# First block of a two-block kernel: S5 preparation on GpSimd, S5 scan between gate projections, convolution and mLSTM last

## The chip, the cores and the metric

The kernel runs on one core of a Trainium2 chip. The metric is the device time of one execution in microseconds (us). The core has five engines that each execute their own instructions in the order in which the program holds them: PE (TensorE, matmuls), DVE (VectorE), ACT (ScalarE), POOL (GpSimd) and SP (SyncE, here only DMA issues). An instruction that has to wait holds up everything behind it on its engine.

## The reference, cut to what matters

The program computes two transformer blocks for S = 256 tokens of width 1024. The change lies in the first third of the first block:

```
h    = rmsnorm(x)
u, q_in, k_in, v, o, i, f, gate = split(h @ w_in)
y_s5 = s5(u)                         # diagonal complex state space, 32 groups x 64 states
y_m  = mlstm(q_in, k_in, v, o, i, f) # q,k: causal convolution of 4 taps, silu; 4 heads, 2 chunks
merged = sigmoid(gate_s5) * (y_s5 @ w_br_s5) + sigmoid(gate_m) * (y_m @ w_br_m)
x = x + merged @ w_out               # then cross attention, FFN, and the second block

s5:  a_bar = exp(lam*dt);  b_bar = (a_bar-1)/lam * b      # depends on parameters alone
     states = associative_scan(a_bar, b_bar u);  y = gelu(Re(c states) + d u);  y * sigmoid(y @ w_glu)
mlstm: per head  p = (q k^T) * decay mask;  h = (w q C + p v) / max(|den|, exp(-m));  norm
```

So three branches (S5, mLSTM, gates) start from the same normalised input and meet in `merged`. Data lets them run in nearly any order.

## The kernel before, in words

**Products.** Every product with a weight matrix is made as three fp32r matmuls. SP loads a raw weight tile of 128 x 1024 (`wload`, L318), ACT rounds it to `hi` (L320), DVE takes `lo` = raw - hi (L321), and PE runs 24 matmuls of 128x256 on the pair (L328, L329, L330; with tokens on the partitions L337 to L339). So every weight tile costs an ACT, a DVE and 24 PE instructions. Four raw and three hi/lo buffers let the loads run ahead.

**Who sets the order.** The Tile scheduler puts each engine's instructions into one list, by the order of the source and by priorities, from simulated times. Weight loads have a raised priority (300), as has `s5_prep` (500).

**First block before.** `s5_prep` (L639 to L723) computes powers of a_bar and the coefficients from parameters, in some 110 small DVE instructions on 128x16 tiles, with two exponentials as POOL `pow` (L306). Then come the norm's statistics (squares, column sums on PE L454, a POOL `pow` `rmsr` L505, `row_bcast` on PE L498), the u projection (w_fm tiles, evacuated by `ev_u` with the factor `rs`), and `s5` (L725): for four groups of heads, outer products of coefficients and parameters (DVE L747 to L762 for `mb` and `w`, POOL L747 to L768 for `mc`, CR and CN), PE transposes (L772) and small matmuls `kp` (L777, L779), the input states (L795), a scan over 64 chunks by ten combine steps of five DVE instructions (L806 to L810), the output matmuls (L830). Program order goes on with the q/k projection and its convolution (`ev_qk`: per pair of tiles one DVE multiply L1646, two ACT instructions, six DVE steps L1654, an ACT tanh L1656, a DVE step L1657), the v, i, f and o projections, `mlstm` (L853 on: gate vectors, then per head scores L914 and L915, mask product `pT` L917, values L919 to L921, normalisation), the eight gate projections (`ev_g`, L1696 and L1698), `s5_glu` (L835, exact fp32 matmuls L424), the branch projections w_brs and w_brm, and w_out.

**Around it.** Since engines follow the lists, in the execution the S5 scan and the four mLSTM heads of DVE lie beside the gate projections of PE: of PE's rows, 27 to 48 gate matmuls stand between the steps of one head and the next.

Of the kernel before, what the change touches and what calls it, by code (L numbers as in the profile page):

```python
# [258 lines left out]
def _program(ctx, tc, nc, a, offs, dump):  # L259
# [379 lines left out]
    def s5_prep(bp):  # L639
        t16 = lambda tag, n=16: T(bp, [P, n], tag)  # L640
        lr, li, ldt = C["lr"], C["li"], C["ldt"]
        dt = pexp(ldt, [P, 16], "s5dt")
# [34 lines left out]
        pr = T(bp, [P, 16, 5], "pr")  # L677
        pi = T(bp, [P, 16, 5], "pi")
        G.memset(pr[:, :, 0:1], 1.0)
        G.memset(pi[:, :, 0:1], 0.0)  # L680
        ar, ai = pr[:, :, 1], pi[:, :, 1]

        def cmul(orr, oi, xr_, xi_, yr, yi):
            n_ = len(orr.shape) > 2 and orr.shape[2] or 1
            sh = list(orr.shape)
            t = [T(bp, sh, "cm%d_%d" % (n_, q_), bufs=2) for q_ in range(4)]
            tt(t[0], xr_, yr, op=mult)
            tt(t[1], xi_, yi, op=mult)
            tt(t[2], xr_, yi, op=mult)
            tt(t[3], xi_, yr, op=mult)  # L690
            tt(orr, t[0], t[1], op=sub)
            tt(oi, t[2], t[3], op=add)

        cs_, sn_ = t16("cs_"), t16("sn_")
        cmul(cs_, sn_, cn, sn, cq, sq)
        tt(ar, er, cs_, op=mult)
        tt(ai, er, sn_, op=mult)
        den, a1 = t16("den"), t16("a1")
        tt(den, lr, lr, op=mult)
        tt(z, li, li, op=mult)  # L700
        tt(den, den, z, op=add)
        V.reciprocal(den, den)
        nli = t16("nli")
        ts(nli, li, -1.0, None, op0=mult)
        cmul(pr[:, :, 2], pi[:, :, 2], ar, ai, ar, ai)
        sq2 = lambda X: bc(X[:, :, 2:3], [P, 16, 2])
        ts(a1, ar, -1.0, None, op0=add)
        cr = T(bp, [P, 16, 4], "cr")
        ci = T(bp, [P, 16, 4], "ci")
        cmul(cr[:, :, 3], ci[:, :, 3], a1, ai, lr, nli)  # L710
        tt(cr[:, :, 3], cr[:, :, 3], den, op=mult)
        tt(ci[:, :, 3], ci[:, :, 3], den, op=mult)
        cmul(cr[:, :, 2], ci[:, :, 2], cr[:, :, 3], ci[:, :, 3], ar, ai)
        cmul(cr[:, :, 0:2], ci[:, :, 0:2], cr[:, :, 2:4], ci[:, :, 2:4], sq2(pr), sq2(pi))
        cmul(pr[:, :, 3:5], pi[:, :, 3:5], pr[:, :, 1:3], pi[:, :, 1:3], sq2(pr), sq2(pi))
        NL = 5
        akr, aki, akn = T(bp, [P, NL, 16], "akr"), T(bp, [P, NL, 16], "aki"), T(bp, [P, NL, 16], "akn")
        V.tensor_copy(akr[:, 0, :], pr[:, :, 4])
        V.tensor_copy(aki[:, 0, :], pi[:, :, 4])
# [4 lines left out]

    def s5(bp, b2, K5, U, prep):  # L725
        cr, ci, pr, pi, akr, aki, akn = prep
        NL = 5
# [14 lines left out]
        def outer(eng, xa, ya, xb, yb, nt, tag):  # L742
            sh = [P, 4, nt, 16]
            m = []
            for x_, y_ in ((xa, ya), (xb, yb)):
                t = T(bp, sh, tag + str(len(m)))
                eng.tensor_tensor(t, bc(x_[:, :, :, None], sh), bc(y_[:, :, None, :], sh), op=mult)  # L747
                m.append(t)
            return m

        halves = [(g, slice(64 * g, 64 * g + 64)) for g in range(2)]
        for b in range(4):
            s4 = slice(4 * b, 4 * b + 4)
            BR, BI = bt[b % 2][:, 0], bt[b % 2][:, 1]
            crb, cib, brb, bib = cr[:, s4, :], ci[:, s4, :], b_re[:, s4, :], b_im[:, s4, :]
            prb, pib, xrb, xib = pr[:, s4, :], pi[:, s4, :], c_re[:, s4, :], c_im[:, s4, :]
            m = outer(V, crb, brb, cib, bib, 4, "mb")
            for g, hs in halves:
                tt(BR[hs, :, :, g, :], m[0][hs], m[1][hs], op=sub)
            m = outer(V, crb, bib, cib, brb, 4, "mb")  # L760
            for g, hs in halves:
                stt(BI[hs, :, :, g, :], m[0][hs], -1.0, m[1][hs], op0=mult, op1=sub)  # L762
            c = outer(G, prb, xrb, pib, xib, 5, "mc")
            for g, hs in halves:
                G.tensor_tensor(CR[hs, s4, :, g, :], c[0][hs], c[1][hs], op=sub)
            c = outer(G, prb, xib, pib, xrb, 5, "mc")
            for g, hs in halves:
                G.tensor_tensor(CN[hs, s4, :, g, :], c[0][hs], c[1][hs], op=add)  # L768
            for src, dst in ((BR, VR), (BI, VI)):
                tr = T(pa, [P, 4, P], "a")  # L770
                for q in range(4):
                    PE.transpose(tr[:, q, :], src[:, q].rearrange("p t g h -> p (t g h)"), ident)  # L772
                ACT.copy(dst[:, s4, :], tr)
            kp = T(pa, [32, 4, P], "a")
            for q in range(4):
                fl = lambda X: X.rearrange("p g h -> p (g h)")
                mm(kp[:, q, :], fl(BR[:, q, 3]), CR[:, 4 * b + q, 0:4].rearrange("p t g h -> p (t g h)"),  # L777
                   start=True, stop=False)
                mm(kp[:, q, :], fl(BI[:, q, 3]), CN[:, 4 * b + q, 0:4].rearrange("p t g h -> p (t g h)"),  # L779
                   start=False, stop=True)  # L780
            for t in range(4):
                ACT.copy(KS[32 * t:32 * t + 32, s4, 32 * t:], kp[:, :, :P - 32 * t])

        us = T(dr, [16, 32, 4, 64], "us")
        U2 = T(bp, [P, 16, 64], "U2")
        nc.scalar.dma_start(us.rearrange("(a j) q t c -> (j q) a (t c)", a=4), U.rearrange("p a t c -> p a (t c)"))
        for t in range(4):
            nc.scalar.dma_start(U2[32 * t:32 * t + 32], us.rearrange("a q t c -> t q a c")[t])
        ST = T(bp, [P, 2, 16, 65], "ST")
        V.memset(ST[:, :, :, 0:1], 0.0)  # L790
        for b in range(4):
            vp = T(pa, [P, 2, 4, 64], "a")
            for r_, W in enumerate((VR, VI)):
                for q in range(4):
                    mm(vp[:, r_, q, :], W[:, 4 * b + q, :], U2[:, 4 * b + q, :], start=True, stop=True)  # L795
            ACT.copy(ST[:, :, 4 * b:4 * b + 4, 1:], vp)

        def combine(k, d0, n_):
# [1001 lines left out]
```

## Time and profile before

| | |
|---|---|
| median of 3 runs | 1218.24 us (1216.67 to 1220.58) |
| profiled execution | 1222.49 us, its span 1220.7 us, mean granted clock 0.980 |
| PE busy | 1175.4 us (96%) |
| DVE busy | 905.4 us (74%) |
| ACT busy | 681.7 us (56%) |
| POOL busy | 94.5 us (8%) in 94 instructions |
| chain that ended last | PE 82%, DVE 11% |

PE is the engine to watch: over the whole program it idles 45 us. The 40-slice line of the page shows where: its first two slices stand at 7 tenths, the slices after them at 9, and the granted clock falls under full speed in the third.

### The profile page before, as it was taken

How to read it: one execution, taken by the hardware profiler on the slowest of the kernel's cores; microseconds unless marked ns; L12 is line 12 of the kernel's file. 1: busy time of each engine (PE TensorE's matmuls, PEld its weight loads, DVE VectorE, ACT ScalarE, POOL GpSimd, SP SyncE). 2: the span in 40 equal slices, each digit the busy share in tenths (PEclk: the TensorE clock that was granted, in tenths of full speed). 3: DMA queues.
4: the chain of work that ended last, by engine and by line, in shares of the span. 5: the costliest groups of instructions: out<-in, count | busy, mean ns of one | idle time of the engine just before them, and what ended most of it. 6: DMA issues, size and time to landing. Idle time of an engine off the chain costs nothing.

```text
span 1220.7 us, 23603 instructions
## 1 busy us (share of the span) xinstructions
PE 1175.4 (96%) x9370; PEld 1111.6 (91%) x9370; DVE 905.4 (74%) x1744; ACT 681.7 (56%) x1205; POOL 94.5 (8%) x94
## 2 busy tenths in 40 slices
PE   7779999999999999999999899999999999999997
PEld 7769989999999999899998899998977789999986
DVE  8998957866689886667564886666687758976654
ACT  5345564755566765446355675554675566755541
POOL 4830000100000000000001000001000001000010
PEclk9979999999999999999999899999998999999998
DMA  7423445664356556656423556566754215666561
GB/s 262 139 87 114 147 137 179 205 202 157 100 177 196 183 177 181 196 175 215 163 79 106 170 173 187 176 181 190 261 182 139 70 54 193 208 188 188 160 201 36
DMA packets 61276, 199.41 MB, mean 163 GB/s; under 512 B 8502, under 2 KB 12398, under 8 KB 60910
## 3 DMA queue, kind: packets, MB, share of 16 engines
q1 hardware_dynamic: 54864, 191.60, 49.5%
q10 hardware_dynamic: 6302, 6.32, 1.6%
q8 instruction: 73, 1.20, 0.4%
q14 instruction: 37, 0.30, 0.1%
HBM read 196.28 MB, written 1.60 MB: 162 GB/s over the span
## 4 chain that ended last, share of the span: by engine, by line
PE 82%; DVE 11%; ACT 2%; DMA 2%; issue 2%; SPq 0%; DVEq 0%; ACTq 0%
PE g L329 10%; PE g L328 10%; PE g L330 10%; PE a L328 7%; PE a L329 7%; PE a L330 7%; PE a L393 5%; PE g L393 4%; DVE lo L321 3%; PE a L395 3%; PE g L337 2%; PE g L339 2%; PE g L338 2%; PE g L395 2%; PE a L947 1%
## 5 line engine op out<-in xcount | busy, mean ns | idle before, releaser
L321 DVE TENSOR_TENSOR lo<-raw,hi 128x1024 fp32r<-128x1024 f32 (+3 forms) x359 | 431.2, 1206 | 180.7 <-ACT hi L320 178.0
L320 ACT CAST hi<-raw 128x1024 fp32r<-128x1024 f32 (+3 forms) x359 | 363.7, 1020 | 355.4 <-PE g L329 138.8
L328 PE MATMUL g<-xh,hi 128*128 128x256 f32 (+1 forms) x616 | 176.2, 287 | 7.9 <-ACT xh L568 7.6
L329 PE MATMUL g<-xl,hi 128*128 128x256 f32 (+1 forms) x624 | 178.9, 287 | 0.3 <-DVE xl L569 0.3
L330 PE MATMUL g<-xh,lo 128*128 128x256 f32 (+1 forms) x616 | 176.3, 287 | 2.7 <-DVE lo L321 2.7
L328 PE MATMUL a<-nh,hi 128*128 128x256 f32 x560 | 159.9, 286 | 4.6 <-ACT sqa L1061 2.7
L329 PE MATMUL a<-nl,hi 128*128 128x256 f32 x560 | 159.5, 285 | 0.9 <-DVE nl L516 0.9
L330 PE MATMUL a<-nh,lo 128*128 128x256 f32 x560 | 159.3, 285 | 0.0
L328 PEld LDWEIGHTS g<-xh,hi 128*128 128x128 f32 x616 | 117.7, 191 | 9.9 <-ACT xh L568 7.9
L330 PEld LDWEIGHTS g<-xh,lo 128*128 128x128 f32 x616 | 117.4, 191 | 4.4 <-DVE lo L321 3.4
L329 PEld LDWEIGHTS g<-xl,hi 128*128 128x128 f32 x624 | 119.0, 191 | 1.4 <-DVE xl L569 0.9
L328 PEld LDWEIGHTS a<-nh,hi 128*128 128x128 f32 x560 | 108.6, 194 | 5.7 <-ACT sqa L1061 2.9
L329 PEld LDWEIGHTS a<-nl,hi 128*128 128x128 f32 x560 | 108.7, 194 | 1.1 <-DVE nl L516 1.1
L330 PEld LDWEIGHTS a<-nh,lo 128*128 128x128 f32 x560 | 108.7, 194 | 0.0
L393 PE MATMUL a<-mx,hi 128*128 128x512 f32 x264 | 91.9, 394 | 0.0
L328 PE MATMUL g<-nh,hi 128*128 128x256 f32 x288 | 81.5, 283 | 0.0
L329 PE MATMUL g<-nl,hi 128*128 128x256 f32 x288 | 81.5, 283 | 0.0
L330 PE MATMUL g<-nh,lo 128*128 128x256 f32 x288 | 81.5, 283 | 0.0
L395 PE MATMUL a<-mx,lo 128*128 128x256 f32 x264 | 73.1, 277 | 0.0
L393 PE MATMUL g<-mx,hi 128*128 128x512 f32 x198 | 69.0, 395 | 0.0
L393 PEld LDWEIGHTS a<-mx,hi 128*128 128x128 f32 x264 | 49.4, 188 | 11.5
L328 PEld LDWEIGHTS g<-nh,hi 128*128 128x128 f32 x288 | 55.3, 192 | 0.0
(619 smaller groups left out, 2905.2 us busy)
## 6 DMA issues: line engine op xcount, KB each, us to landing
raw<-g_up SPq DMA_DIRECT2D x88, 512.0 KB, 3.6
raw<-f_up SPq DMA_DIRECT2D x44, 512.0 KB, 3.5
raw<-g_dn SPq DMA_DIRECT2D x32, 512.0 KB, 3.6
raw<-w_fm SPq DMA_DIRECT2D x27, 512.0 KB, 4.1
raw<-ev_fm SPq DMA_DIRECT2D x20, 512.0 KB, 3.7
raw<-f_dn SPq DMA_DIRECT2D x16, 512.0 KB, 3.6
raw<-od_fm SPq DMA_DIRECT2D x14, 512.0 KB, 4.2
raw<-g_dn SPq DMA_DIRECT2D x16, 384.0 KB, 3.4
```

The lines of the kernel that those rows point to most:

```text
L320: ACT.copy(hi, raw)
L321: tt(lo, raw, hi, op=sub)
L328: mm(ps, hi[:, o:o + P], xh[:, k, :], start=start and k == 0, stop=False, skip_group_check=skip)
L329: mm(ps, hi[:, o:o + P], xl[:, k, :], start=False, stop=False, skip_group_check=skip)
L330: mm(ps, lo[:, o:o + P], xh[:, k, :], start=False, stop=stop and k == kt - 1, skip_group_check=skip)
L337: mm(ps, xh[:, k, t], hi[:, wsl], start=start and j == 0, stop=False, skip_group_check=skip)
L338: mm(ps, xh[:, k, t], lo[:, wsl], start=False, stop=False, skip_group_check=skip)
L339: mm(ps, xl[:, k, t], hi[:, wsl], start=False, stop=stop and j == len(ks) - 1, skip_group_check=skip)
L393: mm(f2, hi[:, o], X[:, k].rearrange("p a s -> p (a s)"), start=first and j == 0, stop=False, skip_group_check=True)
L395: mm(ps[:, 0, :], lo[:, o], X[:, k, 0, :], start=False, stop=last and j == len(ks) - 1, skip_group_check=True)
L947: PE.transpose(tr[:, k, :], b, ident)
```

## The change

Five things change, all in the first block. (1) `s5_prep` is written with complex tiles [128, 2, 16] and runs on POOL; only the reciprocal stays on DVE. Its raised priority goes, and it stands behind the u projection. (2) Buffers are zeroed first (`s5_zero`); POOL keeps KS and CN, two memsets go to DVE. (3) All outer products are on DVE, in two halves of eight groups; ACT scatters the results into CR, CN and the transposes' input. (4) A combine step of the scan has four DVE instructions over the same elements in place of five. (5) The order: u, gates 0 and 1, S5 inputs of the first half, gates 2 and 3, v/i/f, inputs of the second half, v, o, states, gates 4 and 5, scan, gates 6 and 7, mLSTM's gate vectors, q/k projection and convolution, S5 output, mLSTM heads, GLU, branches.

```diff
     def s5_prep(bp):
+        tt, ts = G.tensor_tensor, G.tensor_scalar
...
+        dt = pexp(ldt, [P, 16], "s5dt", G)
+        xt = t2("xt")
+        tt(xt, ll, bc(dt[:, None, :], [P, 2, 16]), op=mult)
...
+        def cmul(o, x_, y_, conj=False):
+            u, v = [T(bp, sh, "cm%d_%d" % (n_, q_), bufs=2 if n_ == 1 else 1) for q_ in range(2)]
+            tt(u, x_, y_, op=mult)
+            tt(v, x_, y_[:, ::-1], op=mult)
...
+                tt(o[:, 0], u[:, 0], u[:, 1], op=sub)
+                tt(o[:, 1], v[:, 0], v[:, 1], op=add)
...
+        return pz, cz, ak, ax
...
+        def outer(xa, ya, xb, yb, nt, op):
+            sh = [P, 8, nt, 16]
+            m = [T(bp, sh, "so", bufs=2), T(bp, sh, "hs")]
+            for t, x_, y_ in ((m[0], xa, ya), (m[1], xb, yb)):
+                tt(t, bc(x_[:, :, :, None], sh), bc(y_[:, :, None, :], sh), op=mult)
+            tt(m[0], m[0], m[1], op=op)
+            return m[0]
+
+        def inputs(b):
+            s8 = slice(8 * b, 8 * b + 8)
...
+            m = outer(pr, xr, pi, xi, 5, sub)
             for g, hs in halves:
+                ACT.copy(CR[hs, s8, :, g, :], m[hs])
...
+            for r_, ops in enumerate(((cr, br, ci, bi, 4, sub), (cr, bi, ci, br, 4, add))):
+                m = outer(*ops)
+                for q in range(2):
+                    for g, hs in halves:
+                        act(bt[q][hs, r_, :, :, g, :], m[hs, 4 * q:4 * q + 4], AF.Copy, scale=1.0 - 2 * r_)
...
-            tt(t1, src, bc(akr[:, k, :][:, None, :, None], [P, 2, 16, n_]), op=mult)
-            tt(t2[:, 0], src[:, 1], ak(aki), op=mult)
-            tt(t2[:, 1], src[:, 0], ak(akn), op=mult)
+            tt(t1, src, bc(ak[:, k, 0][:, None, :, None], sh), op=mult)
+            tt(t2, src[:, ::-1], bc(ax[:, k][:, :, :, None], sh), op=mult)
             tt(dst, dst, t1, op=add)
             tt(dst, dst, t2, op=add)
...
-        with tc.high_priority(500):
-            prep = s5_prep(bp)
+        zero = s5_zero(bp)
...
         gemm_pairs("w_fm", range(2), 8, xh, xl, ev_u, ahead=ahead)
-        y5 = s5(bp, b2, K5, U, prep)
+        prep = s5_prep(bp)
+        s5_inputs, s5_state, s5_scan, s5_output = s5_steps(bp, K5, U, prep, zero)
...
+        gates([0, 1])
+        s5_inputs(0)
+        gates([2, 3])
...
+        gemm_tm("w_vif", range(1), xh, xl, ev_vif, cw=264)
+        s5_inputs(1)
+        gemm_tm("w_tm", range(1, 2), xh, xl, ev_vm)
+        gemm_tm("w_tm", range(2, 4), xh, xl, ev_o)
+        s5_state()
+        gate.append(T(bp, [P, 8, S], "gm"))
+        gates([4, 5])
+        s5_scan()
+        gates([6, 7])
+        mg = mlstm_gates(bp, K5, ifs)
...
         gemm_pairs("w_fm", range(2, 6), 8, xh, xl, ev_qk)
...
+        y5 = s5_output()
+        ymh, yml = mlstm(bp, b2, K5, mg, qk, vm, og)
         ysh, ysl = s5_glu(bp, b2, y5)
```

The lists of three engines show what stands where. On POOL before, from the first exponential on: `s5dt` and `s5er` are the two exponentials of the preparation, `rmsr` is the norm's factor, and `mc` the first outer product.

```order
L306 TENSOR_TENSOR s5dt_122<-ebase_96,early_104 128x16
L473 TENSOR_TENSOR sqa_328<-sq_318,sq_320 128x512
L306 TENSOR_TENSOR s5er_131<-ebase_96,xr_127 128x16
L505 TENSOR_TENSOR rmsr_339<-rmsms_337,mhalf_94 128x2
L747 TENSOR_TENSOR mc_117_491<-pr_169,cs_80_297 128x320
```

On POOL now, the end of the same stretch: `s5er` stands 22 rows ahead of `rmsr` (the last 7 of the rows between are shown), and behind it the preparation goes on.

```order
L670 TENSOR_TENSOR cs_330<-cs_330,z_328 128x16
L675 TENSOR_TENSOR cs_330<-cs_330,z_328 128x16
L644 TENSOR_SCALAR st_305<-cs_330 128x16
L645 TENSOR_TENSOR cs_330<-st_305,z_328 128x16
L672 TENSOR_TENSOR cs_330<-cs_330,r_319 128x16
L644 TENSOR_SCALAR st_305<-cs_330 128x16
L504 TENSOR_TENSOR rmsr_177<-rmsms_175,mhalf_94 128x2
L673 TENSOR_TENSOR cs_330<-cs_330,r_319 128x16
```

`rmsr` moved from right behind `s5er` to behind 21 instructions of the preparation, and the powers `pz` are complete 42 POOL rows after it.

On DVE now, behind the evacuation of u: the outer products `so` and `hs` read the powers `pz` of POOL, and the weight tile `lo_658` (the first of gate pair 2) stands behind three of them.

```order
L320 TENSOR_TENSOR lo_511<-raw_508,hi_510 128x1024
L320 TENSOR_TENSOR lo_541<-raw_538,hi_540 128x1024
L1672 TENSOR_TENSOR mcv_503<-g_442,rs_182 128x512
L760 TENSOR_TENSOR so_572<-pz_358,cs_19_135 128x640
L760 TENSOR_TENSOR so_579<-pz_358,cs_19_135 128x640
L760 TENSOR_TENSOR hs_573<-pz_358,cs_19_135 128x640
L320 TENSOR_TENSOR lo_658<-raw_655,hi_657 128x1024
L761 TENSOR_TENSOR so_572<-so_572,hs_573 128x640
```

Before, no DVE instruction reads the preparation from another engine; here the tile that PE's 198th weight matmul reads waits behind the instructions that do.

On DVE now, at the end of the convolution: `mcv` are its steps for the last two pairs, `w` the evacuation of the S5 output, `x` a finished pair of q/k, `pT` the mask product of the first mLSTM head.

```order
L1733 SCALAR_TENSOR_TENSOR x_1565<-msg_1788,mcv_1779 128x512
L1722 TENSOR_TENSOR msg_1852<-g_1791,rs_182 128x512
L1730 SCALAR_TENSOR_TENSOR mcv_1854<-msg_1852,consts_91,mcv_1854 128x255 x2
L1730 SCALAR_TENSOR_TENSOR mcv_1854<-msg_1852,consts_91,mcv_1854 128x254 x2
L1730 SCALAR_TENSOR_TENSOR mcv_1854<-msg_1852,consts_91,mcv_1854 128x253 x2
L941 SCALAR_TENSOR_TENSOR pT_2083<-a_2080,dm_2076 128x384
L1733 SCALAR_TENSOR_TENSOR x_1565<-msg_1863,mcv_1854 128x512
```

The last pair's convolution now stands right ahead of the first head's `pT`; before, most of the scan stood between the two.

On PE before, at a head: gate matmuls (L328 to L330) stand between the scores (L914, L915) and the values (L919 on) of a head, 43 of them here, of which one is shown on either side.

```order
L914 MATMUL a_1642<-x_998 128x256
L915 MATMUL a_1642<-x_998 128x128
L329 MATMUL g_1915<-xl_300,hi_1918 128x256
...
L329 MATMUL g_1980<-xl_300,hi_1983 128x256
L919 MATMUL a_1647<-vm_1299,pT_1645 128x129
L920 MATMUL a_1647<-vm_1299,pT_1645 128x129
```

On PE now, at the first two heads (scores L938 and L939, values L943 to L945, L929 spreads a gate vector, L423 is the GLU):

```order
L423 MATMUL g_2241<-w_305_1866,raw_2242 128x256 x5
L938 MATMUL a_2080<-x_1565 128x256
L939 MATMUL a_2080<-x_1565 128x128
L943 MATMUL a_2085<-vm_784,pT_2083 128x129
L944 MATMUL a_2085<-vm_784,pT_2083 128x129
L945 MATMUL a_2085<-vm_784,pT_2083 128x129
L929 MATMUL a_2099<-M_1548,consts_91 128x256
L938 MATMUL a_2107<-x_1565 128x256
L939 MATMUL a_2107<-x_1565 128x128
L327 MATMUL g_2258<-KS_2221,hi_2261 128x256
L327 MATMUL g_2290<-KS_2221,hi_2293 128x256
L943 MATMUL a_2112<-vm_784,pT_2110 128x129
```

The gate matmuls that stood between scores and values are gone from there: none stands in the first head, two matmuls of w_brs in the second, 19 in the third and 34 in the fourth.

## Rows read from the trace of the kernel before

**Rows 1.** The page, part 1 and the engines of part 4

```profile
PE 1175.4 (96%) x9370; PEld 1111.6 (91%) x9370; DVE 905.4 (74%) x1744; ACT 681.7 (56%) x1205; POOL 94.5 (8%) x94
...
PE 82%; DVE 11%; ACT 2%; DMA 2%; issue 2%; SPq 0%; DVEq 0%; ACTq 0%
```

**Rows 2.** Busy time by window; columns: window, its length, each engine, PEclk, DMA, GB/s

```profile
0.00:21.90 21.90, 13.93 (x84) 13.11 (x85) 18.35 (x50) 13.05 (x21) 13.44 (x17) 1.00 0.85 298
0.00:100.00 100.00, 78.05 (x575) 73.18 (x576) 92.15 (x232) 47.90 (x80) 50.49 (x51) 0.91 0.50 160
100.00:220.00 120.00, 117.96 (x1267) 113.40 (x1267) 96.47 (x173) 65.22 (x118) 3.86 (x3) 1.00 0.46 150
```

**Rows 3.** Waits of PE, 0 to 300 us; columns: us in total, times, longest

```profile
PE g L338 <- DVE lo L321: 8.0, 2, 6.8
PE g L328 <- ACT xh L568: 7.6, 1, 7.6
PE g L330 <- DVE lo L321: 2.7, 3, 1.7
PE a L772 <- DVE w L759: 2.1, 1, 2.1
```

**Rows 4.** Busy time by window, a stretch of weight matmuls and the slow one

```profile
30.00:35.00 5.00, 5.00 (x45) 5.00 (x44) 5.00 (x23) 2.15 (x3) 0.00 (x0) 1.00 0.72 231
60.00:75.00 15.00, 7.36 (x31) 5.88 (x32) 14.88 (x31) 2.16 (x4) 10.85 (x12) 0.50 0.12 41
```

**Rows 5.** Timeline of POOL, 0 to 35 us; columns: start, duration, instruction, idle before

```profile
12.51 2.92 POOL L306 TENSOR_TENSOR s5er<-ebase,xr 128x16 f32<-128x16 f32 x1 [1.45 <-DVE th L645]
23.24 0.69 POOL L505 TENSOR_TENSOR rmsr<-rmsms,mhalf 128x2 f32<-128x2 f32 x1 [7.82 <-ACT rmsms L503]
```

**Rows 6.** Timeline of DVE, 12 to 15 us

```profile
12.70 1.22 DVE L321 TENSOR_TENSOR lo<-raw,hi 128x1024 fp32r<-128x1024 f32 x1
13.84 0.17 DVE L650 TENSOR_SCALAR n<-n 128x16 f32<-128x16 f32 x1
```

**Rows 7.** Timeline of DVE and POOL about 680 us, a later layer norm

```profile
679.01 1.23 DVE L321 TENSOR_TENSOR lo<-raw,hi 128x1024 fp32r<-128x1024 f32 x1 [0.83 <-ACT hi L320]
...
679.61 0.68 POOL L1038 TENSOR_TENSOR lnv<-lnmu 128x2 f32<-128x2 f32 x1 [13.85 <-ACT lnmq L1036]
...
680.37 0.19 POOL L1039 TENSOR_TENSOR lnv<-lnmq,lnv 128x2 f32<-128x2 f32 x1
...
680.64 0.71 POOL L1041 TENSOR_TENSOR lnr<-lnv,mhalf 128x2 f32<-128x2 f32 x1
```

**Rows 8.** DVE by form, 20 to 76 us; columns: busy, mean ns, idle

```profile
L691 DVE TENSOR_TENSOR akr<-cm,cm 128x16 f32<-128x16 f32 x4 | 2.4, 598 | 0.0
...
L691 DVE TENSOR_TENSOR cr<-cm,cm 128x16 f32<-128x16 f32 x2 | 0.3, 172 | 0.0
```

**Rows 9.** DVE by line, 100 to 152 us

```profile
L810 DVE TENSOR_TENSOR ST<-ST,w 128x1024 f32<-128x1024 f32 (+9 forms) x10 | 7.0, 705 | 0.0
L809 DVE TENSOR_TENSOR ST<-ST,w 128x1024 f32<-128x1024 f32 (+9 forms) x10 | 7.0, 696 | 0.0
L806 DVE TENSOR_TENSOR w<-ST,akr 128x1024 f32<-128x1024 f32 (+9 forms) x10 | 6.9, 693 | 2.7 <-ACT ST L796 2.6
L807 DVE TENSOR_TENSOR w<-ST,aki 128x512 f32<-128x512 f32 (+9 forms) x10 | 4.2, 417 | 0.0
```

**Rows 10.** DVE by form, 76 to 101 us

```profile
L1654 DVE SCALAR_TENSOR_TENSOR mcv<-msg,consts,mcv 128x254 f32<-128x254 f32 x4 | 1.8, 478 | 0.0
...
L1657 DVE SCALAR_TENSOR_TENSOR x<-msg,mcv 128x512 f32<-128x512 f32 x2 | 1.4, 693 | 0.9 <-ACT msg L1656 0.8
```

**Rows 11.** PE alone by window, where L830 of the S5 output runs

```profile
152.50:157.90 5.40, 3.86 (x234) 1.00 0.63 201
```

**Rows 12.** PE by line, 100 to 205 us

```profile
L424 PE MATMUL g<-w,raw 128*128 128x256 f32 x32 | 7.2, 379 | 0.0
```

More of the change, by code (lines that the diff above doesn't have):

```diff
@@ L676, in s5_prep @@
         tt(sq, sq, j, op=mult)
[L677 to L701, printed above, removed]
-        V.reciprocal(den, den)
[L703 to L715, printed above, removed]
+        pz = T(bp, [P, 2, 16, 5], "pz")
@@ L739, in s5, with s5_steps @@
+    def s5_steps(bp, K5, U, prep, zero):
+        pz, cz, ak, ax = prep
+        CR, CN, KS, bt, ST = zero
+        NL = 5
+        VR = T(xp, [P, 16, P], "x")
+        VI = T(bp, [P, 16, P], "gm")
         g16 = lambda nm: K5[nm].rearrange("p (j h) -> p j h", h=16)
         b_re, b_im, c_re, c_im = g16("b_re"), g16("b_im"), g16("c_re"), g16("c_im")
[L742 to L749, printed above, removed]
@@ L758, in s5 @@
             for g, hs in halves:
-                tt(BR[hs, :, :, g, :], m[0][hs], m[1][hs], op=sub)
-            m = outer(V, crb, bib, cib, brb, 4, "mb")
+                ACT.copy(CR[hs, s8, :, g, :], m[hs])
+            m = outer(pr, xi, pi, xr, 5, add)
             for g, hs in halves:
[L762 to L770, printed above, removed]
-                for q in range(4):
[L772 to L780, printed above, removed]
@@ L781, in s5 @@
-            for t in range(4):
[L782 to L796, printed above, removed]
+                ACT.copy(CN[hs, s8, :, g, :], m[hs])
+            for r_, ops in enumerate(((cr, br, ci, bi, 4, sub), (cr, bi, ci, br, 4, add))):
[3 more added lines that the diff above has]
+                        act(bt[q][hs, r_, :, :, g, :], m[hs, 4 * q:4 * q + 4], AF.Copy, scale=1.0 - 2 * r_)
@@ new lines, in inputs @@
+            for q4 in range(2):
+                s4 = slice(8 * b + 4 * q4, 8 * b + 4 * q4 + 4)
+                BR, BI = bt[q4][:, 0], bt[q4][:, 1]
+                for src, dst in ((BR, VR), (BI, VI)):
+                    tr = T(pa, [P, 4, P], "a")
+                    for q in range(4):
+                        PE.transpose(tr[:, q, :], src[:, q].rearrange("p t g h -> p (t g h)"), ident)
+                    ACT.copy(dst[:, s4, :], tr)
+                kp = T(pa, [32, 4, P], "a")
+                for q in range(4):
+                    fl = lambda X: X.rearrange("p g h -> p (g h)")
+                    jj = 8 * b + 4 * q4 + q
+                    mm(kp[:, q, :], fl(BR[:, q, 3]), CR[:, jj, 0:4].rearrange("p t g h -> p (t g h)"),
+                       start=True, stop=False)
+                    mm(kp[:, q, :], fl(BI[:, q, 3]), CN[:, jj, 0:4].rearrange("p t g h -> p (t g h)"),
+                       start=False, stop=True)
+                for t in range(4):
+                    ACT.copy(KS[32 * t:32 * t + 32, s4, 32 * t:], kp[:, :, :P - 32 * t])
@@ new lines, in s5_steps, with state @@
+        box = {}
+        def state():
+            us = T(dr, [16, 32, 4, 64], "us")
+            U2 = box["U2"] = T(bp, [P, 16, 64], "U2")
+            nc.scalar.dma_start(us.rearrange("(a j) q t c -> (j q) a (t c)", a=4),
+                                U.rearrange("p a t c -> p a (t c)"))
+            for t in range(4):
+                nc.scalar.dma_start(U2[32 * t:32 * t + 32], us.rearrange("a q t c -> t q a c")[t])
+            for b in range(4):
+                vp = T(pa, [P, 2, 4, 64], "a")
+                for r_, W in enumerate((VR, VI)):
+                    for q in range(4):
+                        mm(vp[:, r_, q, :], W[:, 4 * b + q, :], U2[:, 4 * b + q, :], start=True, stop=True)
+                ACT.copy(ST[:, :, 4 * b:4 * b + 4, 1:], vp)
@@ L835, in s5, with scan, output @@
-        dump("s5y", y)
-        return y
+        def scan():
+            for k in range(NL):
+                combine(k, 2 << k, 64 >> (k + 1))
+            for k in range(NL - 1, -1, -1):
+                n_ = (64 >> (k + 1)) - 1
+                if n_:
+                    combine(k, 3 << k, n_)
+        def output():
+            U2 = box["U2"]
+            y = T(bp, [P, 4, S], "w40")
+            Y4 = T(bp, [P, 4, 4, 64], "w41")
+            for b in range(2):
+                yp = T(pa, [P, 2, 4, 64], "a")
+                for k in range(2 * b, 2 * b + 2):
+                    for t in range(4):
+                        for step in range(3):
+                            for j in range(4):
+                                jj = 4 * k + j
+                                w = (KS[:, jj, 32 * t:32 * t + 32] if step == 0
+                                     else (CR, CN)[step - 1][:, jj, t + 1].rearrange("p g h -> p (g h)"))
+                                v = U2[:, jj, :] if step == 0 else ST[:, step - 1, jj, 0:64]
+                                mm(yp[32 * j:32 * j + 32, k % 2, t, :], w, v, start=step == 0, stop=step == 2,
+                                   skip_group_check=True)
+                    Y = Y4[:, k]
+                    stt(Y, U[:, k], C["s5_d"][:, k:k + 1], yp[:, k % 2], op0=mult, op1=add)
+                    act(y[:, k, :].rearrange("p (c t) -> p t c", t=4), Y, AF.Gelu_apprx_tanh)
+            dump("s5y", y)
+            return y
@@ L838, in s5_glu @@
+        return inputs, state, scan, output
     def s5_glu(bp, b2, y):
```

190 lines of the change are left out of this document (95 added, 95 removed).

## The prediction

> **What bounds the kernel now.** I read the page first, then the windows of the first 220 us, the waits of PE there, and last the timelines of single instructions. PE is busy 96% of the span and holds 82% of the chain that ended last [rows 1], so the time changes only where PE waits, or runs at less than full clock. The change touches the stretch from 0 to about 220 us. There PE is busy 78.05 of the first 100 us and 117.96 of the next 120 [rows 2]: idle 21.95 and 2.04 us. Of the first part 7.6 us are the start, a wait for the first activations [rows 3] that the change leaves as it is. The other 14.3 us are waits for DVE: for weight tiles `lo` (8.0 and 2.7) and for S5 outer products (2.1 the largest) [rows 3]. DVE is busy 92.15 of the first 100 us [rows 2], so it sets the pace there. From 60 to 75 us the granted clock was 0.50 [rows 4], the lower of the two levels (1.2 and 2.4 GHz), after those waits had thinned out PE's work; its 7.36 us busy there would have taken half: 3.7 us lost. So a perfect order could give back 14.3 + 3.7 + 2.0 = 20.0 us. The question is what the new order puts in their place.
>
> **The change part by part.**
>
> Outer products: DVE's work in the first stage falls by the preparation (some 110 small instructions, of .172 us alone and .598 while POOL runs a large one [rows 8]) and rises by POOL's share of the outer products. The waits on `w` and on late `lo` tiles go, since the inputs now lie between many more weight tiles. I count all 20.0 us as saved, and price what is new apart.
>
> `rmsr` behind the preparation: it was waiting for its own input, 7.82 us of POOL idle, and started at 23.24 [rows 5]. Now 21 preparation instructions stand between `s5er` and it. `s5er` ended at 15.4 [rows 5] after a wait for DVE of 1.45 us that goes, so 14.0. A dependent short POOL instruction takes .27 us from start to start (680.37 to 680.64) when DVE is quiet, and .76 (679.61 to 680.37) when a DVE `lo` is under way [rows 7]. 21 x .27 = 5.7 gives 19.7. DVE holds a `lo` of 1.14 us start to start [rows 6] for each 24 weight matmuls, which take 24 x 5/45 = 2.67 us [rows 4]: 43% of the time. If POOL stands still in all of it, 5.7 becomes 10.0. Midway, and with `rmsr`'s .69, the result is there at about 23.0. PE's list wants `row_bcast` behind 76 weight matmuls, and in the trace 84 PE records were over by 21.9 [rows 2]. New wait 1.2 us (0 to 4).
>
> `pz` and the tile behind it: `pz` is 42 POOL rows later: 42 x .27 = 11.3, so 34.3 with no hindrance and 23.0 + 11.3/.57 = 42.8 if POOL stands still under every `lo`. I take the middle, 38.5, since only a POOL instruction that meets a `lo` is held and `lo` tiles come in bursts. On DVE three outer products of 640 elements (between .69 for 512 [rows 10] and 1.23 for 1024 [rows 7], so some .75) and `lo_658` itself of 1.14 follow: 41.9. PE reaches that tile after 122 more matmuls, 23.1 + 122 x .111 = 36.6. So a new wait of 5.3 us (1.1 to 9.6). The tiles queued on DVE behind the waiting `so` all come late with it; buffers for three tiles cover one of them. The remaining 19 preparation rows on POOL stretch later outer products and ACT has the scatter copies: 1.5 us more (0 to 3). If the wait thins out PE enough for the clock to fall as it did at 60 us, up to 3.7 is lost again; I take 1.5.
>
> By the Trainium skill (SBUF — State Buffer, "Who interferes with whom") the port pair of DVE and GpSimd is an exclusive lock that the first comer keeps for the whole instruction when DVE has two SBUF inputs. Rows 7 agree: the `lnv` that began .60 us into a `lo` ended at 680.29, with the `lo` at 680.24. Rows 5 and 6 speak for a weaker form, since a `lo` at 12.70 took its usual 1.22 us under the `pow` of 12.51 to 15.43. By the rule in full `pz` would stand at 42.8 and the sum be 4.3 us higher.
>
> The middle: from the S5 states on DVE has 40 scan instructions over the elements of the 50 before. Records overlap by some .08 (the 1.22 us `lo` of 12.70 is followed at 13.84 [rows 6]). The scan is 7.0 + 7.0 + 6.9 + 2 x 4.2 = 29.3 (the pair of L807 has the same size) [rows 9], less 50 x .08, so 25. With it, ahead of the first head's `pT`, stand 16 `lo` of 1.14 (18.2), 24 convolution steps of .40 (9.6), 11 instructions of 512 elements of .61 (6.7) [rows 6, 10], four evacuations of the S5 output (1.6) and 15 small ones (1.7): 62.8 us. PE has in the same stretch 384 weight matmuls (42.7), the S5 output (5.4 [rows 11]), the GLU (7.2 [rows 12]) and small ones (1.2): 56.5. DVE is 6.3 us late at the first head. Before, PE had gate matmuls there, some 43 between the scores and the values of a head; now it has none. New wait 6.3 us (0 if the convolution of the last pairs finds DVE free, 10 if ACT's steps of the convolution add to the chain). DVE, on the other hand, idles ahead of the states, where it has little left: its load is only moved.
>
> The heads and the end: in the second head two matmuls stand where DVE needs about 5 us for the first head's rest and the next `pT` (x .61, arg .4, two message and merge steps of .61, hs .6, pT .55 and ACT between): 3.0 us. The third and fourth have 19 and 34 matmuls (2.1 and 3.8 us) and are covered. Behind the last head the norm needs a `pow` of 8 columns on POOL (between .69 and 2.92 for 2 and 16 columns [rows 5]) and transposes; 41 matmuls cover 4.6 of an estimated 6.7: 2.1 us. The m branch now ends right ahead of w_out, so that its last evacuation and the first product of w_out are exposed, estimated at 3.1. Clock after these gaps 1.5 (0 to 4). Tail: 6.3 + 3.0 + 2.1 + 3.1 + 1.5 = 16.0 (3 to 22).
>
> Sum: -20.0 + (1.2 + 5.3 + 1.5 + 1.5) + 16.0 = +5.5 us on the profiled execution's 1222.49, so 1228.0. That execution lies 4.25 us over the median 1218.24 of the runs, and against these I expect 1223.7.
>
> **The rivals.**
>
> A, faster. The scan and the convolution fit beside PE and the first preparation is quick: `pz` by 34.3, early costs 1.2 + 1.1 + .5, tail about 7. -20.0 + 9.8 = -10.2: 1208. For it: DVE's share in all of 100 to 220 us is 96.47 of 120 [rows 2], so there is slack on average, and POOL was nearly idle. Against it: the lists put the whole convolution and four S5 evacuations of DVE between the last gate matmul and the first head.
>
> B, no change that can be told. The early gain and the late loss cancel: early costs of 5, tail of 13, -2: 1216 to 1220. For it: both depend on the same 62.8 against 56.5, where 5% of either is 3 us.
>
> C, clearly slower, one mechanism: POOL against DVE. If every preparation row costs .76 as in the held case [rows 7], the 42 rows take 32 us, `pz` stands at 55, `lo_658` at 58.4, and PE waits 21.8 instead of 5.3: +22, so 1240. It decides from about .45 us a row on, where the early wait passes what the old one cost. Against it: DVE waits for POOL then and stops hindering it, so the chain frees itself.
>
> D, the change does not do what it says: the lists show that it does; a chance of nothing worth counting.
>
> **How the numbers follow.** Less than 0.3% (3.7 us) cannot be told from no change here, so faster means under 1214.6 and slower over 1221.9. The forecast has .37 (its own range 1222 to 1232), A .28, B .27, C .08. Faster .28, same .27, slower .45. The range runs from A's 1207 to 1236, with some of C and the best end of A left out.
>
> **What would show it.** Right: the clock at 1.00 from 50 to 100 us; a wait of PE on a `lo` at 36 to 43 us with DVE waiting for POOL in `so`; waits of PE on `pT` at the first two heads with DVE busy all through the convolution. Wrong: DVE idle ahead of the first `pT`, or PE busy 19.5 of 20 us in every window to 220, or POOL's preparation over by 34 us. The prediction falls as a whole if the tail's waits sum to under 8 us.

## The result: 1.1% slower, and what the profile shows after the change

The changed kernel takes 1232.47 us (median of 4 runs, 1229.66 to 1233.40) against 1217.53 of the kernel before in the same comparison: ratio 1.0113, 95% interval 1.0098 to 1.0129. The forecast was slower by 5.5 us; it is slower by 14.9. The profiled executions lie nearer together, 1232.13 against 1222.49, so 9.6 us of it can be looked up in the traces.

The page of the kernel after, part 1, and PE's busy tenths and the clock in its 40 slices, with these two lines of the kernel before below them:

```profile
PE 1180.7 (96%) x9370; PEld 1115.6 (91%) x9370; DVE 884.8 (72%) x1628; ACT 692.6 (56%) x1227; POOL 97.0 (8%) x145
...
PE   6999888799999999999999899999999999999997
...
PEclk9999989899999999999999989999998999999999
```

```profile
PE   7779999999999999999999899999999999999997
...
PEclk9979999999999999999999899999998999999998
```

PE's busy time is 5.3 us longer than in [rows 1] for the same 9370 matmuls; half clock took 9.4 us of the first 250, against 4.7 before. Before, three slices stood at 7 tenths (three, not two as said above), the clock being low in the third; after, the first stands at 6 and slices 5 to 8 at 7 and 8. The windows that answer to [rows 2] (columns as there):

```profile
0.00:100.00 100.00, 88.27 (x694) 85.26 (x695) 67.90 (x109) 63.68 (x110) 48.62 (x102) 0.98 0.55 175
100.00:140.00 40.00, 40.00 (x335) 38.81 (x334) 39.86 (x67) 17.16 (x22) 3.10 (x1) 1.00 0.45 151
140.00:160.00 20.00, 15.24 (x421) 13.40 (x421) 15.37 (x30) 11.75 (x18) 3.66 (x1) 0.91 0.38 124
160.00:180.00 20.00, 17.05 (x81) 14.08 (x79) 11.74 (x30) 9.23 (x28) 0.00 (x0) 0.83 0.17 53
180.00:200.00 20.00, 17.35 (x141) 16.56 (x141) 13.32 (x28) 8.99 (x22) 1.78 (x1) 1.00 0.33 106
200.00:220.00 20.00, 17.96 (x145) 17.14 (x143) 12.87 (x18) 7.63 (x11) 0.00 (x0) 1.00 0.55 184
220.00:240.00 20.00, 13.66 (x89) 13.36 (x90) 13.90 (x21) 11.95 (x20) 1.27 (x1) 0.74 0.39 119
```

The first 100 us are better by 10 us of PE time (88.27 busy against 78.05), 100 to 140 us are full. From 140 us on every window is short, and the clock falls twice, at 140 to 180 and 220 to 240. The waits of PE to 300 us, which answer to [rows 3]:

```profile
PE g L327 <- ACT xh L567: 8.0, 1, 8.0
PE g L327 <- ACT hi L319: 6.4, 2, 6.1
PE g L329 <- DVE lo L320: 3.7, 3, 1.7
PE g L423 <- ACT w L852: 3.1, 2, 2.4
PE a L962 <- DVE hn L961: 2.7, 2, 2.5
PE g L327 <- ACT KS L517: 2.3, 1, 2.3
PE m L497 <- POOL rmsr L504: 2.0, 1, 2.0
PE a L848 <- DVE w L851: 1.7, 1, 1.7
PE a L943 <- DVE pT L941: 0.7, 1, 0.7
```

The waits for S5 outer products are gone and those for `lo` have fallen from 10.7 to 3.7 us. New are waits for the GLU's input (L423), its output (KS), the norm of the heads (hn), and one of 6.1 us for a weight tile `hi`.

To compare kernels, I add up PE's loss by stage, from windows of 5 us: idle time, plus what half clock cost (busy time x (1 - granted clock)). The start's wait of some 8 us is in every first column, and each figure is rounded by itself.

| kernel | 0 to 50 us | 50 to 140 | 140 to 200 | 200 to 250 | sum | ratio to before (95%) |
|---|---|---|---|---|---|---|
| before | 10.3 | 16.4 | 1.6 | 0.7 | 29.0 | 1 |
| after | 13.2 | 0.1 | 15.1 | 11.4 | 39.8 | 1.0113 (1.0098 to 1.0129) |
| e1_qk_first | 13.3 | 9.2 | 0.9 | 0.8 | 24.2 | 0.9969 (0.9950 to 0.9989) |
| e2_mem_later | 13.8 | 0.1 | 14.9 | 2.8 | 31.5 | 1.0067 (1.0044 to 1.0089) |
| e3_prep_dve | 8.5 | 0.0 | 14.9 | 9.3 | 32.7 | 1.0044 (1.0028 to 1.0060) |
| e4_gates_filler | 13.2 | 4.1 | 7.0 | 3.2 | 27.5 | 1.0018 (1.0004 to 1.0032) |
| e5_dve_filler | 8.9 | 4.1 | 8.0 | 1.6 | 22.5 | 0.9949 (0.9933 to 0.9966) |
| e6_state_early | 8.4 | 2.1 | 11.0 | 0.4 | 21.9 | 0.9948 (0.9926 to 0.9971) |
| e9_qk_first_dve | 8.5 | 5.7 | 5.1 | 0.4 | 19.7 | 0.9910 (0.9882 to 0.9938) |
| e10_pool_same_place | 14.8 | 7.6 | 0.7 | 0.8 | 23.9 | 0.9942 (0.9927 to 0.9957) |
| e11_outers_pool | 10.8 | 13.0 | 1.3 | 0.8 | 25.8 | 0.9943 (0.9923 to 0.9962) |
| e12_inputs_later | 9.1 | 6.2 | 1.9 | 0.4 | 17.6 | 0.9888 (0.9871 to 0.9904) |

The sums and the ratios agree within 6 us. A sum is of one profiled execution, a ratio of all runs; and behind 250 us, where all these kernels have the same work, the profiled executions idle for 19 to 21 us and lose 6.5 to 11.4 us through the clock.

### The profile page after: what moved, and what is told of

It reads as the page before. It is cut to its first block, busy times and chain, and to the rows that moved or that the text cites. A ratio compares the mean times of both kernels' runs of the same rounds, so it can differ in the third digit from the quotient of the medians.

```text
span 1230.3 us, 23548 instructions
## 1 busy us (share of the span) xinstructions
PE 1180.7 (96%) x9370; PEld 1115.6 (91%) x9370; DVE 884.8 (72%) x1628; ACT 692.6 (56%) x1227; POOL 97.0 (8%) x145
## 4 chain that ended last, share of the span: by engine, by line
PE 75%; DVE 4%; ACT 2%; issue 1%; DMA 0%; DVEq 0%; ACTq 0%
PE g L328 9%; PE g L327 9%; PE g L329 9%; PE a L327 7%; PE a L328 7%; PE a L329 7%; PE a L392 5%; PE g L392 4%; PE a L394 2%; PE g L394 2%; PE g L338 2%; PE g L336 2%; PE g L337 1%; DVE lo L320 1%; PE a L971 1%; PE m L1160 1%
## 5 line engine op out<-in xcount | busy, mean ns | idle before, releaser
L328 PE MATMUL g<-xl,hi 128*128 128x256 f32 (+1 forms) x624 | 180.5, 290 | 0.0
L328 PE MATMUL a<-nl,hi 128*128 128x256 f32 x560 | 159.3, 285 | 0.9 <-DVE nl L515 0.9
L328 PEld LDWEIGHTS g<-xl,hi 128*128 128x128 f32 x624 | 120.7, 193 | 1.1 <-DVE xl L568 0.6
L328 PEld LDWEIGHTS a<-nl,hi 128*128 128x128 f32 x560 | 108.6, 194 | 1.1 <-DVE nl L515 1.1
L328 PE MATMUL g<-nl,hi 128*128 128x256 f32 x288 | 81.5, 283 | 0.0
```

What stands on the lines that cost most here:

```text
L328: mm(ps, hi[:, o:o + P], xl[:, k, :], start=False, stop=False, skip_group_check=skip)
```

## The experiments

**e1: the old order of projections with the new parts.** q/k first and the gates last (lines that only move are left out; a tile of the S5 inputs, `VR`, goes to another buffer, since q/k takes its own):

```diff
-        gates([0, 1])
+        gemm_pairs("w_fm", range(2, 6), 8, xh, xl, ev_qk)
         s5_inputs(0)
-        gates([2, 3])
...
         s5_state()
...
-        gates([4, 5])
         s5_scan()
-        gates([6, 7])
         mg = mlstm_gates(bp, K5, ifs)
...
+        gates(list(range(8)))
```

> The changed kernel's parts (preparation on GpSimd, outer products on DVE, four-step scan), but the program order of before for the projections: u, q/k and convolution, S5 inputs, v/i/f, v, o, states, scan, S5 output, mLSTM, then all eight gate pairs. Theory L (the loss is in the late part, where no gate matmuls are left to stand beside the convolution, the scan and the heads): PE's idle time from 140 to 240 us falls from 18.7 us to about 3 and the clock stays at 1.00 there, the early part keeps its gain, so about 1205 us. Rival E (the loss comes from the new parts themselves, POOL's preparation above all): with the old order the time stays at 1225 or above.

Measured 1213.66 us. The late loss (from 140 us on) falls from 26.6 to 1.7 us: in its main point theory L holds, the order makes the late loss. But the early part doesn't keep its gain, as L had it: the early loss is 22.5 us against 13.2 after the change, so the time is 9 us above the forecast of 1205. What the four-step scan, or the zeroing ahead, is worth by itself was not run.

**e2: the load of the memory tokens later.**

```diff
         mem = T(ap_, [P, 8, S], "mem")
+        V.tensor_copy(mem[:, 0:2, 0:1], x1[:, 0:2, 0:1])
```

> The changed kernel with one edge more: the load of the memory tokens for the cross attention waits until the first pair of w_out is evacuated, so that ACT's list holds one weight tile of w_out behind the memory's split instead of four. Theory M (PE's wait of 6.05 us at 220 us, and the clock of 0.50 to 0.76 behind it, come from ACT standing at a memory load that lands late, with w_out's weight tiles behind it in its list): about 9 us faster, 1223 us. Rival: the memory is late in any case and the wait only moves to the k projection: 1230 to 1233 us.

Measured 1226.48 us, 6.0 less than after the change (5.6 by the ratios). The rows show why the wait had been there. ACT's list after the change, where `oh` is the memory's split and `hi` are weight tiles of w_out (the memory's squares stand between):

```order
L319 CAST hi_2624<-raw_2622 128x1024
L567 ACTIVATE oh_2792<-mem_2790,consts_91 128x256 x8
...
L319 CAST hi_2656<-raw_2654 128x1024
```

Four of w_out's eight tiles stand behind the memory's work; in the kernel before two did, and there ACT waited .49 us for the load and PE .3:

```profile
215.01 3.31 ACT L568 ACTIVATE oh<-mem,consts 128x256 fp32r<-128x256 f32 x8 [0.49 <-DMA mem<-mem]
```

After the change, the load itself, on SP's queue (columns: start, time in the queue):

```profile
211.82 0.33 SPq L976 DMA_DIRECT2D mem<-mem  x1
```

and ACT then (columns: start, duration, instruction, idle before):

```profile
219.42 3.30 ACT L567 ACTIVATE oh<-mem,consts 128x256 fp32r<-128x256 f32 x8 [4.87 <-DMA mem<-mem]
...
224.80 2.93 ACT L319 CAST hi<-raw 128x1024 fp32r<-128x1024 f32 x3
```

and PE:

```profile
225.88 0.58 PE L327 MATMUL g<-xh,hi 128*128 128x256 f32 x1 [6.05 <-ACT hi L319]
```

The load was issued at 211.82, once DVE had written the last part of the merge (`xl` L518, the releaser of SP there), and landed 7.5 us later; ACT stood still for 4.87 us and PE for 6.05. With the edge (the added copy writes part of `x1`, the first pair of w_out, into `mem`, and the load has to wait for it), PE by window (columns as in [rows 2]) is:

```profile
220.00:225.00 5.00, 5.00 (x44) 5.00 (x44) 2.48 (x5) 2.06 (x4) 0.00 (x0) 1.00 0.94 360
225.00:230.00 5.00, 4.08 (x33) 3.68 (x31) 4.62 (x11) 5.00 (x11) 0.63 (x1) 1.00 0.35 130
```

and without it, in the changed kernel:

```profile
220.00:225.00 5.00, 0.00 (x0) 0.00 (x0) 4.42 (x10) 5.00 (x13) 1.16 (x1) 0.71 0.00 1
225.00:230.00 5.00, 3.66 (x15) 3.36 (x16) 4.83 (x6) 2.72 (x3) 0.10 (x1) 0.50 0.35 107
```

PE is busy 9.08 of 10 us with the edge and 3.66 without, the clock 1.00 against .71 and .50, the latter the lower of its two levels. The loss of 200 to 250 us falls from 11.4 to 2.8, 8.6 us in these two executions; the time falls by 6 of the 9 us that theory M gave. So M holds for the cause, and its size is some two thirds in the time.

**e3: the preparation on DVE again, e10: its engine alone.** e3 takes DVE's functions in place of GpSimd's and the old place and priority. e10 takes the kernel e9 below and changes the engine alone:

```diff
-        tt, ts = V.tensor_tensor, V.tensor_scalar
+        tt, ts = G.tensor_tensor, G.tensor_scalar
```

> The changed kernel with the S5 preparation on DVE again, at the place and priority that it had before, all else as changed. Theory L: the preparation on GpSimd is a gain or neutral, so this one is the same or slower, 1232 to 1240 us, with DVE busier in the first 40 us. Rival E (the preparation on GpSimd costs, through the waits for its factor and powers and the port that it shares with DVE): 1222 to 1227 us.

> The run with q/k first and the preparation on DVE, with nothing changed but the preparation's engine, GpSimd in place of DVE, at the same place and priority. In the runs so far engine and place changed together. Theory S (a dependent chain of 88 short instructions at .3 us each on GpSimd against .1 us on DVE, with DVE standing in its list until it is done): early idle and clock loss up by some 8 us, 1213 to 1217 us. Rival (the cost came from the place in the program, behind the u projection): 1206 to 1210 us, as with DVE.

Measured: e3 1223.31 us, so rival E was right there: with 85 instructions more on DVE (1713 against 1628 in the pages; the 88 above is a miscount) the early loss falls to the 8.5 us of the start alone. e10 gives 1212.24 against 1207.86 of e9: 4.4 us for the engine alone, half of theory S's 8 and .8 us under its range. By the ratios it is 3.9, and their intervals overlap, so the times alone don't settle it. The traces do for the early part: up to 140 us the loss is 22.4 in e10 and 14.2 in e9, the 8 us of theory S. Some 4 come back at 140 to 200 us, where PE in e9 stands 2.35 us at the S5 output for nothing that the profile shows, with 1.7 us of half clock there. The place made no difference to the early loss: in e1, which differs from e10 by place and priority alone, it is 22.5 (times of 0.9969 and 0.9942 of before, with intervals that overlap). What GpSimd took is in the timeline of e10. DVE:

```profile
37.60 1.64 DVE L760 TENSOR_TENSOR so<-pz,cs 128x640 f32<-128x640 f32 x2 [5.07 <-POOL pz L702]
...
39.94 1.27 DVE L320 TENSOR_TENSOR lo<-raw,hi 128x1024 fp32r<-128x1024 f32 x1
```

GpSimd in e10, the last two instructions of the powers:

```profile
37.31 0.25 POOL L702 TENSOR_TENSOR pz<-cm 128x32 f32<-128x32 f32 x1
37.52 0.26 POOL L703 TENSOR_TENSOR pz<-cm 128x32 f32<-128x32 f32 x1
```

and of e9 on DVE:

```profile
36.41 1.22 DVE L320 TENSOR_TENSOR lo<-raw,hi 128x1024 fp32r<-128x1024 f32 x1
...
37.94 0.18 DVE L702 TENSOR_TENSOR pz<-cm 128x32 f32<-128x32 f32 x1
38.04 0.18 DVE L703 TENSOR_TENSOR pz<-cm 128x32 f32<-128x32 f32 x1
```

The powers are ready at the same time, 37.8 and 38.2 us. But DVE does weight tiles and convolution between the preparation's instructions in e9, and in e10 stands 5.07 us at the first outer product with all of them behind it. An instruction takes .2 to .3 us from start to start on GpSimd, .10 on DVE.

**e4 and e5: gate pairs as company for the heads.**

```diff
         s5_state()
...
-        gates([4, 5])
         s5_scan()
-        gates([6, 7])
...
         ymh, yml = mlstm(bp, b2, K5, mg, qk, vm, og)
...
+        gates([4, 5, 6, 7])
```

> The changed kernel with gate pairs 4 to 7 moved in program order from around the scan to behind the mLSTM heads, so that their 192 matmuls stand beside the convolution's rest and the heads; scan before the q/k projection as changed. Theory L: PE's waits between 148 and 195 us (10.3 us idle, and some 5 us of half clock) fall to under 4 us: about 1220 us. Rival D (DVE's 62 us of scan, convolution and weight tiles are the bound whatever stands beside them): the waits move to the q/k projection, 1229 to 1234 us.

> The changed kernel with both the preparation on DVE (as in the run with that alone) and gate pairs 4 to 7 behind the heads in program order (as in the run with that alone). If the two terms are separate and add up: idle and clock loss 8.5 us up to 140 us plus 4 for the scan's start, 10 us behind it, against 29 us of the kernel before, so about 1212 us. If they are one cost seen twice (DVE's total load): 1218 to 1221 us, as with the better of the two.

Measured 1220.49 and 1212.81 us. In e4 the loss of 140 to 200 us is halved (15.1 to 7.0), but 4 us come back ahead of it while DVE scans, as rival D has it. And the loss behind 200 us falls from 11.4 to 3.2, one more of w_out's tiles standing ahead of the memory's work. So of the 12.3 us that e4 loses less, the heads' new company brings 4.1 and the memory load 8.2: that the time is L's 1220 is luck, since L did not reckon with the memory. L and D each hold in part. Of the waits that are left, the largest at the scan and the heads are DVE's:

```profile
PE a L943 <- DVE pT L941: 3.2, 1, 3.2
...
PE g L327 <- DVE ST L823: 1.4, 1, 1.4
PE g L327 <- DVE msg L1719: 1.4, 1, 1.4
```

In e5 both gains add up as forecast (0.0069 and 0.0095 of the time before, together 0.0164).

**e6: states ahead of v and o.** `s5_state()`, the q/k projection and `s5_scan()` ahead of the v and o projections, else as e5.

> As the run before it, and the S5 states, the q/k projection and the scan moved ahead of the v and o projections, so that DVE's scan and convolution start some 15 us earlier and v, o and the gate pairs 4 to 7 stand beside them. If the late loss is a matter of DVE's work coming too late against PE's list: idle behind 100 us under 6 us, about 1208 us. If DVE is now short early (preparation, outer products and convolution in the first 90 us): waits for weight tiles there as in the kernel before, 1214 to 1219 us.

Measured 1212.19 us, like e5 and not the 1208 of the first theory: the loss of 140 to 200 us grew from 8.0 to 11.0, where 50 to 140 us gained 2. The largest waits of PE there are for a head's mask from ACT (`dm`, 3.6 us) and for `pT` (1.9). Whether an earlier scan could pay is open.

**e9: e1 with the preparation on DVE.**

> The run with the program order of before (q/k first, gates last) and the new parts, but the preparation on DVE. It asks what the engine of the preparation is worth where no gate matmuls fill the early part. If the preparation costs more on GpSimd than on DVE in any order: faster than that run, 1206 to 1211 us. If GpSimd pays off where DVE is the bound of the early part: slower, 1217 to 1222 us.

Measured 1207.86 us, inside the first expectation, and 0.9% faster than the kernel before: of the preparation only the two `pow` and two memsets are on GpSimd, as they were before. (What is said above, that before the change no DVE instruction reads the preparation from another engine, leaves these two `pow` out.)

**e11: GpSimd for some of the outer products.** In e9, the products for CR and CN (12 of the 24 instructions, not the 24 of 48 of the expectation; one of two lines is shown):

```diff
-            m = outer(pr, xr, pi, xi, 5, sub)
+            m = outer(pr, xr, pi, xi, 5, sub, G.tensor_tensor)
```

> The run with q/k first and the preparation on DVE, with the outer products for CR and CN (24 of 48 DVE instructions, those of 640 elements and their combination) on GpSimd, as half of them were before. Theory P (large GpSimd instructions beside DVE slow both, so that GpSimd is no help while DVE is busy): DVE's small instructions lengthen as before the change (.6 against .17 us), 1213 to 1219 us. Rival (DVE's load is what counts, and 9 us of it leave): 1203 to 1207 us.

Measured 1212.71 us, 4.8 slower than e9 and just short of theory P's range; by the ratios 4.0, with intervals that overlap a little. In the traces the early loss is 23.8 us against 14.2. A convolution step of DVE, 30 to 80 us (busy, mean ns), in e11:

```profile
L1679 DVE SCALAR_TENSOR_TENSOR mcv<-msg,consts,mcv 128x253 f32<-128x253 f32 x6 | 6.1, 1026 | 0.0
```

in e9:

```profile
L1679 DVE SCALAR_TENSOR_TENSOR mcv<-msg,consts,mcv 128x253 f32<-128x253 f32 x6 | 2.8, 475 | 0.0
```

and one of GpSimd's own in e11, 30 to 100 us:

```profile
L760 POOL TENSOR_TENSOR so<-pz,cs 128x640 f32<-128x640 f32 x4 | 6.9, 1739 | 28.5 <-DVE pz L702 18.5 <-ACT w L778 10.1
```

The convolution step beside it is twice as long (1026 against 475 ns), and a product that takes DVE .82 us in e9 takes GpSimd 1.7. By the Trainium skill (SBUF — State Buffer, "SBUF: two separate sides") GpSimd and a DVE instruction with two SBUF inputs share a port pair, which whichever starts first holds for its whole instruction if GpSimd's reads SBUF, too; these rows agree.

**e12: the S5 inputs one projection later** (`s5_inputs(0)` behind v/i/f, `s5_inputs(1)` behind v, else e9).

> The run with q/k first and the preparation on DVE, with the two halves of the S5 inputs one projection later (behind v/i/f and behind v). If the remaining early waits there (4.2 us about 51 to 55 us and 1.7 us of clock) come from the outer products standing ahead of the weight tiles and factors of v/i/f: 1202 to 1206 us. If the inputs are needed by then and the scan starts later for it: 1208 to 1211 us.

Measured 1206.57 us, ratio 0.9888: the fastest, though not clear of e9 (their intervals overlap), and above the range of its first expectation. What that theory asked for did not happen: the wait of 2.6 us for `ifs` stayed, and the early loss is 15.3 us against 14.2. In its trace less is lost at 140 to 200 us (1.9 against 5.1), where e9 has the 2.35 us that the profile doesn't explain.

## Why the prediction was right in its direction and too small in size

- **What the change saves (20.0 us): right, as far as it can be told apart.** The waits of [rows 3] for S5 and the slow clock of [rows 4] are gone; 50 to 140 us lose 0.1 us in place of 16.4.
- **`rmsr` (at 23.0, wait 1.2): right.** It ended at 22.57 + .73 = 23.3, and PE waited 2.0. (The terms that the prediction gives add up to 22.5, not 23.0.)

```profile
14.82 1.06 POOL L657 TENSOR_SCALAR n<-xt 128x16 f32<-128x16 f32 x1
...
19.92 0.22 POOL L668 TENSOR_TENSOR z<-r 128x16 f32<-128x16 f32 x1
...
22.57 0.73 POOL L504 TENSOR_TENSOR rmsr<-rmsms,mhalf 128x2 f32<-128x2 f32 x1
...
37.66 0.25 POOL L703 TENSOR_TENSOR pz<-cm 128x32 f32<-128x32 f32 x1
```

- **`pz` (38.5): right, its wait too large.** It was ready at 37.9, close to the value midway between no hindrance and all; most instructions took .2 to .4 us, those that met a `lo` 1.1 to 1.3 (the one at 14.82 met the first row below). DVE waited for it 3.3 us. The tile behind it was there at 41.35, as foreseen (41.9), but PE's wait for it was 1.7 us where 5.3 were foreseen, since PE came to it at 39.7 and not at 36.6: it had lost .8 us more at `rmsr` and 1.5 us through the clock behind that wait, and its matmuls came .118 us apart (next point). Early sum: 5.2 us beyond the start against 9.5. Two of the signs of being right came with it: this wait on a `lo`, and the clock at 1.00 from 50 to 100 us.

```profile
14.59 1.22 DVE L320 TENSOR_TENSOR lo<-raw,hi 128x1024 fp32r<-128x1024 f32 x1
...
37.74 1.64 DVE L760 TENSOR_TENSOR so<-pz,cs 128x640 f32<-128x640 f32 x2 [3.30 <-POOL pz L702]
...
40.08 1.27 DVE L320 TENSOR_TENSOR lo<-raw,hi 128x1024 fp32r<-128x1024 f32 x1
```

```profile
41.40 0.38 PE L329 MATMUL g<-xh,lo 128*128 128x256 f32 x1 [1.70 <-DVE lo L320]
```

- **The first two heads (6.3 + 3.0): near in size, but by luck; the mechanism was another.** The forecast has DVE late since it has 62.8 us of work beside PE's 56.5. From the scan's first instruction to the first head's `pT` the trace has (columns as in [rows 2]):

```profile
95.69:164.75 69.06, 64.27 (x812) 60.52 (x810) 63.39 (x106) 31.16 (x44) 6.76 (x1) 0.98 0.39 130
```

DVE's work is as forecast, 63.4 us, but PE's is 64.3 (1.4 of it half clock), so DVE has hardly a surplus of work. (One part of it: I took .111 us a matmul from 45 in 5 us [rows 4], a count that includes those at the window's ends; from start to start it is .118.) DVE stood idle for 5.7 of these 69.1 us, most of it for ACT's steps of the convolution (2.5), a late `hi` (1.5) and a `pow` (1.2). That is the prediction's own sign of being wrong, DVE idle ahead of the first `pT`. PE waited .65 us on `pT`; before and behind it, it waited at the evacuation of the S5 output (1.7), the GLU's input (3.1) and the GLU's output (2.3): 7.8 us together. I had counted the S5 output and the GLU as PE's cover, and they were themselves waiting. The GLU's input shows for what: DVE had written the S5 output's first part at 148.63, but ACT stood 2.39 us for a weight tile of w_brs, cast it and loaded a table before its activation `w`. ACT, then PE:

```profile
149.84 1.04 ACT L319 CAST hi<-raw 128x1024 fp32r<-128x1024 f32 x1 [2.39 <-DMA raw<-w_brs]
150.90 1.28 ACT L852 ACT_TABLE_LOAD   x1
152.20 0.66 ACT L852 ACTIVATE w<-w 128x256 f32<-128x256 f32 x1
```

```profile
152.91 0.70 PE L423 MATMUL g<-w,raw 128*128 128x256 f32 x2 [2.44 <-ACT w L852]
```

- **The end (2.1 + 3.1): near.** `hn` 2.7, the waits at w_out's start 1.8. No row stands behind the 6.7 us of the norm or the 3.1, so the agreement shows little.
- **The step that failed is the tail's sum (16.0), in two terms: clock 1.5 and nothing for the memory load.** From 140 to 250 us PE lost 26.6 us. 18.8 are idle time, of which 6.5 are the memory load that ACT's list puts ahead of four tiles of w_out (6.05, and .47 for the next `lo`); in e2 the idle time of 200 to 250 us falls from 8.4 to 2.8. 7.8 are half clock: 4.8 between 150 and 180 us, behind 4.8 us of idle time in 145 to 155 and 2.9 in 160 to 170, and 3.0 between 220 and 235, behind the memory's, which e2 takes away whole. The prediction gives no working for its 1.5, though [rows 4] had a price: 7.64 us idle and 3.68 lost through the clock in the same 15 us. As an estimate from that, the 14.5 us of gaps that it foresaw would have cost some 7. It is no fixed price: in e4 4.0 us of idle time at 50 to 140 us cost nothing through the clock. The lists held the memory load: `oh` stands ahead of the last tiles of w_out, and its load waits for the end of the merge.
- **Two errors offset each other.** The tail cost 10.6 us more than its 16.0, and 4.3 of that are hidden by the early waits, which cost 5.2 and not 9.5.
- **The rest of the miss is which execution was profiled.** On the profiled executions the forecast was +5.5 and the result +9.6. I took 4.25 us off because the profiled execution of before lay that much over its median; the profiled execution of after lay 0.3 under its own, and the median of before is 0.7 lower in this comparison. These make the remaining 5.3 us.
- **Rival A and the preparation's engine.** That the scan would hide beside PE was wrong after the change; with the gates behind the heads the late loss is 1.7 us in e1 and 5.5 in e9. And GpSimd, which I priced at 9.5 us early and as a loss only by its waits, costs some 4 us as an engine between e9 and e10, 8 in the early part of their traces.

## What to carry to other kernels

Matmuls that depend on nothing late are the stuff that covers the waits of a vector stage; spent early, on a stage that another engine can no longer speed up, they are missing where the dependent chain ends, and a tail of small gaps can cost again through the clock (here 7.8 us beside 18.8). An idle engine is no free place for a chain of short instructions: count what it takes per instruction there, and what stands behind the first reader of its result in the list of the busy engine. After any such move, read every engine's list up to the next stage's loads: a load that waits for the end of this stage holds up whatever stands behind its first reader.

## What had not been expected of the hardware

A `pow` on GpSimd of 2.9 us did not stretch the `lo` of DVE that began beside it [rows 5, 6], while tensor products of 640 elements doubled DVE's steps (e11). In e9 a `pow` that began at 13.00, .07 us into a `lo`, took 3.93 us, and the next `lo`, at 14.66 and under that `pow`, its usual 1.21. So the cost of GpSimd beside DVE is not a matter of how long its instruction runs. Why a `pow` leaves DVE alone was not tried.
